# v of four pairs at once with the sequence in the partitions, twelve merge gates moved into the pairs

## The chip, the cores and the metric

The kernel runs on one core of a Trainium2 chip. The core has five engines that work side by side: TensorE (PE, matmuls into PSUM banks), VectorE (DVE), ScalarE (ACT), GpSimd (POOL) and SyncE (SP), whose queue issues nearly all DMAs of this kernel, in order. The metric is the time of one execution on the device in microseconds (us), as the median of several runs.

## The reference

One layer of a decoder with three branches; sequence 1024, width 1024, float32:

```python
h = rms_norm(x, norm_g[l])
proj = jnp.einsum('bsd,dn->bsn', h, w_in[l])
(a_val, a_glu, a_gate, b_q, b_f, b_i, b_gate,
 c_q, c_k, c_v, c_gate, c_f, merge) = jnp.split(proj, split_points, axis=-1)
ya = conformer_conv(a_val, a_glu, ...) * jax.nn.silu(a_gate)
yb = hgrn2(b_q, b_f, b_i, lower_bounds[l], hgrn_norm_g[l]) * jax.nn.silu(b_gate)
yc = forgetting_attention(c_q, c_k, c_v, c_f + fox_f_bias[l], ...) * jax.nn.silu(c_gate)
branches = jnp.stack([ya, yb, yc], axis=2)
branch_d = jnp.einsum('bskc,kcd->bskd', branches, w_branch[l])
gates = jax.nn.sigmoid(merge.reshape(B, S, N_BRANCH, D_MODEL))
x = x + jnp.einsum('bsd,de->bse', jnp.sum(gates * branch_d, axis=2), w_out[l])
```

Branch a is a causal depthwise convolution of width 31 with a LayerNorm over the channels behind it, branch b a gated linear recurrence (hgrn), branch c attention with a forget gate. c_v and b_i are the "v" of branches c and b. The merge gates are 3 x 1024 columns of the projection.

## The kernel before

**Jobs.** h is kept transposed (channels in the partitions) as a high and a low part, hT_hi and hT_lo. A projection of 128 columns is a *job*: 48 matmuls of 128x512, in two halves of 24 (high x high, high x low, low x high, for eight blocks of channels). Its weights are loaded by `fetch` (tile wraw, 512 KB) and taken apart by `split`: ScalarE copies the high part whi, VectorE subtracts to get the low part wlo; each of the three tiles has two buffers. `lin` walks through the list of 137 full jobs in order. Their results rotate over three PSUM banks, bank0 to bank2, one per half, so a half can start when the half three before it is out of its bank.

**Stages.** First eight pairs (head pair c of attention with head c of hgrn), eight jobs each: q, k, v and gate of c, then q, f, v and gate of b. Then the convolution (glu and val, eight channel blocks), mixed with the merge gates m_c and the branch matmuls br_c; then m_b and br_b; then the gates of branch a (ag0 to ag7), m_a0 to m_a7, br_a0 to br_a7; at the end the output projection.

**What runs beside the jobs.** Coroutines (attention `att`, `hgrn`, the turning of v `vprep`, `conv`, `lnstats`, `yload`) issue their steps in between. A planner (`Sched`) with costs per engine decides when each goes on, and a scheduler then sets the final order of every engine. Free tiles of 128x1056 come from a pool `F` of 18; a tile can be given out again only when its last readers, stores among them, are done.

**v.** A v job leaves v with channels in the partitions; `v_done` copies it out of the banks, `vprep` turns it by eight 128x128 transposes on TensorE into two extra banks, and ScalarE copies it out again. Then attention or hgrn of that pair starts.

**Convolution and LayerNorm.** `conv` takes 31 steps per channel block on VectorE, adds the result to a sum and stores it in zdram. `lnstats` follows the last block: GpSimd adds the sum over the partitions (`partition_all_reduce`, line 928), ScalarE makes the mean, and then each of the eight blocks is loaded, the mean is subtracted, it is stored again, squared and added up, on two tiles in turn; a second sum over the partitions (line 946) and a few steps give rs, the factor that every y of branch a is multiplied with.

**Gates of a.** `ag_done` takes each half of an ag job out of its bank by a tanh on ScalarE and an operation on VectorE; behind the second half come six more VectorE operations that need rs and end in the high and low part of that block, yhi and ylo.

**Branches.** `yload` brings yc (and later yb) from memory into ylo, ScalarE copies the high part to yhi, VectorE subtracts. A branch job br needs its gate (`merge_done`, tanh of an m job), and for b and a the sum so far from mdram; br_b stores its sum in mdram by halves.

**Opening.** x comes in eight tiles on SP's queue; per tile ScalarE squares, VectorE scales, TensorE turns. g8 (the norm's weights), gq, gk and fb are loaded on ScalarE's queue; g8 is turned, and VectorE copies it to gcol (line 1225).

## Time and profile before

| | us |
|---|---|
| median of 3 runs (1909.35 to 1914.12) | 1911.22 |
| the profiled execution | 1909.62 |
| its span | 1907.9 |
| TensorE busy | 1887.4 (99%) |
| VectorE busy | 1284.9 (67%) |
| ScalarE busy | 954.0 (50%) |
| GpSimd busy | 187.5 (10%) |

The stages by job starts: opening to 45 us, the pairs to 1017 (124 us each), convolution with branch c to 1378, branch b to 1553, the gates of a to 1640, m_a to 1727, br_a to 1814, output to 1908.

Busy time counts an instruction's whole record. Records of matmuls overlap, so the distance between starts says more than their length. The chain of waits goes back from the last instruction to what released each step; a wait named there is one that counted.

### The profile page before, as it was taken

The page shows a single profiled execution, that of the slowest core. Times are in us where ns is not written, and L with a number is a line of the kernel's source. Part 1 is how long each engine was busy: PE and PEld are TensorE (multiplying, and loading weights), DVE is VectorE, ACT ScalarE, POOL GpSimd, SP SyncE. Part 2 cuts the span into 40 slices and gives each one's busy share as a digit, 9 for nine tenths or more (in the row PEclk, how much of TensorE's full clock was granted, in tenths as well). Part 3 has the DMA queues.
Part 4 walks back from the last instruction along what each step waited for, and adds up shares of the span by engine and source line. Part 5 has one row for each costly group of instructions (what it writes and reads, how often), then busy time and mean ns, then how long its engine had stood idle before and what let it go on. Part 6 is the DMA issues. An engine that isn't in the chain of part 4 may idle for free.

```text
span 1907.9 us, 27045 instructions
## 1 busy us (share of the span) xinstructions
PE 1887.4 (99%) x11083; PEld 1551.7 (81%) x11083; DVE 1284.9 (67%) x1692; ACT 954.0 (50%) x1508; POOL 187.5 (10%) x164
## 2 busy tenths in 40 slices
PE   7999999999999999999999999999999999999999
PEld 6887878878878788787887888888888888888888
DVE  6566595775756857659577999999996467413431
ACT  5767768767687687776876411111121234322210
POOL 2021120211202111112021100000000110000000
PEclk9999999999999999999999999999999999999999
DMA  4111111111111111111111322222344553313441
GB/s 147 45 34 45 45 34 45 56 35 56 32 39 53 34 45 45 45 47 32 45 56 41 137 75 70 67 77 67 123 153 151 196 158 92 88 45 102 119 128 49
DMA packets 173012, 140.83 MB, mean 74 GB/s; under 512 B 4909, under 2 KB 155445, under 8 KB 172888
## 3 DMA queue, kind: packets, MB, share of 16 engines
q1 hardware_dynamic: 172520, 139.10, 23.5%
q8 instruction: 87, 1.43, 0.3%
q14 instruction: 37, 0.30, 0.0%
q10 hardware_dynamic: 368, 0.01, 0.0%
HBM read 109.72 MB, written 29.36 MB: 73 GB/s over the span
## 4 chain that ended last, share of the span: by engine, by line
PE 86%; ACT 8%; DVE 3%; DMA 2%; issue 1%; POOL 0%; DVEq 0%; SPq 0%; ACTq 0%; POOLq 0%
PE bank L111 84%; ACT fb L124 4%; ACT khi L124 2%; DVE fa L128 1%; PE bank L115 1%; DMA zdram<-fa 1%; ACT L124 1%; ACT fa L124 1%; DMA fa<-zdram 1%; ACT whi L354 0%; PE bank L1246 0%; PE bank L1223 0%; DVE wlo L355 0%; DVE fb L128 0%; DVE klo L132 0%
## 5 line engine op out<-in xcount | busy, mean ns | idle before, releaser
L111 PE MATMUL bank<-hT_hi,whi 128*128 128x512 f32 x1792 | 706.9, 394 | 0.0
L111 PE MATMUL bank<-hT_hi,wlo 128*128 128x512 f32 x1792 | 701.3, 391 | 0.6 <-DVE wlo L355 0.5
L111 PE MATMUL bank<-hT_lo,whi 128*128 128x512 f32 x1792 | 701.0, 391 | 0.0
L111 PEld LDWEIGHTS bank<-hT_hi,wlo 128*128 128x128 f32 x1792 | 336.5, 188 | 72.0 <-issue 2.4
L111 PEld LDWEIGHTS bank<-hT_hi,whi 128*128 128x128 f32 x1792 | 336.8, 188 | 69.3 <-issue 3.2
L111 PEld LDWEIGHTS bank<-hT_lo,whi 128*128 128x128 f32 x1792 | 336.9, 188 | 64.2 <-issue 0.2
L354 ACT ACTIVATE whi<-wraw 128x1024 fp32r<-128x1024 f32 x137 | 144.9, 1058 | 355.5 <-PE bank L111 341.0
L132 DVE SCALAR_TENSOR_TENSOR fa<-fa,taps,fa 128x1024 f32<-128x1024 f32 x240 | 299.1, 1294 | 0.4
L355 DVE TENSOR_TENSOR wlo<-wraw,whi 128x1024 fp32r<-128x1024 f32 x137 | 191.6, 1399 | 126.4 <-ACT whi L354 125.6
L128 DVE TENSOR_TENSOR fa<-fa,fa 128x512 f32<-128x512 f32 (+3 forms) x226 | 173.4, 782 | 66.5 <-ACT fa L124 49.6
L124 ACT ACTIVATE fa<-bank 128x512 f32<-128x512 f32 (+1 forms) x182 | 103.3, 576 | 141.3 <-PE bank L111 128.1
L111 PE MATMUL bank<-yhi,whi 128*128 128x512 f32 x384 | 149.4, 389 | 0.0
L111 PE MATMUL bank<-ylo,whi 128*128 128x512 f32 x384 | 149.2, 389 | 0.0
L111 PE MATMUL bank<-yhi,wlo 128*128 128x512 f32 x384 | 149.2, 389 | 0.0
L124 ACT ACTIVATE fb<-bank 128x512 f32<-128x512 f32 (+5 forms) x262 | 114.1, 450 | 41.2 <-PE bank L111 29.8
L128 DVE TENSOR_TENSOR fa<-fa,fb 128x512 f32<-128x512 f32 (+1 forms) x121 | 81.4, 672 | 58.9 <-ACT fb L124 37.8
L124 ACT ACTIVATE fb<-bank,negF,rk 128x256 f32<-128x256 f32 (+1 forms) x184 | 89.2, 549 | 49.1 <-PE bank L111 33.4
L124 ACT ACT_TABLE_LOAD x83 | 106.5, 1283 | 4.3 <-DVE fb L128 2.9
L132 DVE SCALAR_TENSOR_TENSOR fa<-fa,bank 128x512 f32<-128x512 f32 x96 | 65.4, 682 | 59.8 <-PE bank L111 59.7
L124 ACT ACTIVATE fa<-fa 128x256 f32<-128x256 f32 (+3 forms) x109 | 75.8, 720 | 53.4 <-DMA zdram<-fa 28.2
L124 ACT ACTIVATE fb<-fb 128x1024 f32<-128x1024 f32 (+2 forms) x96 | 88.1, 952 | 16.1 <-DVE fb L128 15.1
L111 PEld LDWEIGHTS bank<-yhi,wlo 128*128 128x128 f32 x384 | 72.1, 188 | 15.1
(163 smaller groups left out, 2136.1 us busy)
## 6 DMA issues: line engine op xcount, KB each, us to landing
wraw<-in_w_in_dram SPq DMA_DIRECT2D x113, 512.0 KB, 3.7
wraw<-in_w_branch_dram SPq DMA_DIRECT2D x24, 512.0 KB, 3.7
zdram<-fa SPq DMA_DIRECT2D x16, 512.0 KB, 4.0
mdram<-fa SPq DMA_DIRECT2D x32, 256.0 KB, 2.0
fa<-mdram SPq DMA_DIRECT2D x16, 512.0 KB, 3.5
fa<-zdram SPq DMA_DIRECT2D x16, 512.0 KB, 3.3
...
```

Source lines behind the costliest of these rows:

```text
L111: self.nc.tensor.matmul(out, lhsT=lhsT, rhs=rhs, start=start, stop=stop)
L115: self.nc.tensor.transpose(out, in_, ident)
L124: return self.nc.scalar.activation(out, in_, func, **kw)
L128: self.nc.vector.tensor_tensor(out=out, in0=a, in1=b, op=op)
L132: self.nc.vector.scalar_tensor_tensor(out=out, in0=a, scalar=s, in1=b, op0=op0, op1=op1)
L354: pin(nc.scalar.activation(j.hi, j.raw, AF.Copy))
L355: pin(eng.tensor_tensor(out=j.lo, in0=j.raw, in1=j.hi.bitcast(F32), op=ALU.subtract))
```

## The change

- **v.** Four jobs of a new kind, all in the first pair, replace the 16 v jobs. A `VJob` makes v of four pairs of one branch: the stationary side is a block of hT (128 positions of the sequence), the moving side 512 columns of weights. Its weights are loaded, copied and subtracted by `vfetch` in eight tiles of F; `vgroup` runs eight groups of 24 matmuls. The result has the sequence in the partitions and goes to memory (vdram). Each pair loads its v from there in `g_pre`, and attention and hgrn of a pair start there. `vprep` is gone.
- **Gates.** The twelve jobs m_b2 to m_b7 and m_a2 to m_a7 run inside pairs 1 to 7 (pairs 1 to 5 take two, 6 and 7 one) and their tanh is stored in gdram; `br_pre` loads it. So a pair has eight jobs up to pair 5, and seven in the last two (counted from 0).
- **hgrn's keys** are turned by seven transposes, not eight.
- **Opening.** g8, gq, gk and fb are loaded on SP's queue, between the tiles of x; the turn of g8 and the copy to gcol stand behind the scaling of the fourth tile.

The diff, cut:

```diff
+    def vfetch(j):
+        yield need(KT + 2)
+        j.lo = [F.get(dt=F32R, w=S) for _ in range(4)]
+        j.hi = [F.get(dt=F32R, w=S) for _ in range(4)]
+        for n, (lo, hi) in enumerate(zip(j.lo, j.hi)):
+            raw = F.get()
+            nc.sync.dma_start(out=raw[:, 0:S].rearrange("p (k c) -> p k c", k=2),
...
+                nc.scalar.activation(hi[:, 0:S], raw[:, 0:S], AF.Copy)
+                nc.vector.tensor_tensor(out=lo[:, 0:S], in0=raw[:, 0:S],
...
+    def vgroup(j):
+        w = lambda ts, k: ts[k // 2][:, k % 2 * H2:(k % 2 + 1) * H2]
+        for i in range(KT):
+            if i % 2 == 0:
+                yield need(1)
+                ot = F.get()
+            ps = ps_lin()
+            for k in range(KT):
+                hh, hl = (h[:, k, i * P:(i + 1) * P] for h in hT)
+                sc.mm(ps, hh, w(j.hi, k), k == 0, False, 228)
+                sc.mm(ps, hh, w(j.lo, k), False, False, 228)
+                sc.mm(ps, hl, w(j.hi, k), False, k == KT - 1, 228)
...
+            sc.act(ot[:, i % 2 * H2:(i % 2 + 1) * H2], ps, AF.Copy)
...
-    def vprep(st, tag, cb):
-        vT, V = st["vT"], st["V"]
-        yield
-        pss = yield from bget(2)
-        for k in range(KT):
-            sc.tr(pss[k // 4][:, k % 4 * P:(k % 4 + 1) * P], vT[:, k * P:(k + 1) * P], ident)
-        for half in range(2):
-            sc.act(V[:, half * H2:(half + 1) * H2], pss[half], AF.Copy)
...
+            nc.sync.dma_start(out=st["V"][:, 0:S], in_=vdram[tag, c // 4][c % 4])
+            st["v"] = True
             cb()
...
-        for ch in range(KT):
+        for ch in range(KT - 1):
             sc.tr(pss[ch // 4][:, ch % 4 * P:(ch % 4 + 1) * P], k_in[:, ch * P:(ch + 1) * P], ident)
...
+            if (b, j) in gdram:
+                yield need(1, True)
+                mg[b, j] = F.get(True)
+                nc.sync.dma_start(out=mg[b, j][:, 0:S], in_=gdram[b, j])
...
+        def done(half, hs, ps):
+            sc.act(st["t"][:, hs], ps, AF.Tanh, scale=0.5)
+            if half == 1:
+                nc.sync.dma_start(out=gdram[b, j], in_=st["t"][:, 0:S])
+                fput(st["t"])
...
-        if j + AHB < KT:
+        if j + AHB < KT and ("b", j + AHB) not in gdram:
             jobs.append(mjob("b", j + AHB))
...
-    jobs += [mjob("a", j) for j in range(KT)]
+    jobs += [mjob("a", j) for j in range(KT) if ("a", j) not in gdram]
...
+    K(nc.tensor.transpose(banks[7][:, 0:KT], g8, ident[0:KT, 0:KT]))
+    K(nc.vector.tensor_copy(gcol, banks[7][:, 0:KT]))
```

The order of three engines at three places. First VectorE's queue where rs becomes ready, before: the first row ends in rs (fa5_307), the last one empties the first half of ag0 from bank1 (fa7_348).

```order
L128 TENSOR_TENSOR fa5_307_9496<-fa5_307_9496,fa8_342_11921 128x1024
L355 TENSOR_TENSOR wlo_12159<-wraw_12084,whi_12158 128x1024
L128 TENSOR_TENSOR fa9_345_11951<-fa9_345_11951,fa3_347_12090 128x512
L128 TENSOR_TENSOR fa0_350_12177<-fa0_350_12177,fa5_307_9496 128x1024
L128 TENSOR_TENSOR fa2_354_12247<-fa2_354_12247,fa5_307_9496 128x1024
L136 TENSOR_SCALAR fa6_351_12178<-fa0_350_12177,vecs_110 128x1024
L132 SCALAR_TENSOR_TENSOR fa7_348_12175<-fa1_349_12176,bank1_77 128x512
```

The same place in the new order: the first row ends in rs (fa4_368), the last one empties the first half of ag2 from bank2.

```order
L129 TENSOR_TENSOR fa4_368_10234<-fa4_368_10234,fa7_405_12385 128x1024
L129 TENSOR_TENSOR fa0_410_12439<-fa0_410_12439,fa4_368_10234 128x1024
L129 TENSOR_TENSOR fa3_414_12509<-fa3_414_12509,fa4_368_10234 128x1024
L137 TENSOR_SCALAR fa6_411_12440<-fa0_410_12439,vecs_110 128x1024
L137 TENSOR_SCALAR fa9_415_12510<-fa3_414_12509,vecs_110 128x1024
L133 SCALAR_TENSOR_TENSOR fa6_411_12440<-fa8_409_12438,fa6_411_12440 128x1024
L133 SCALAR_TENSOR_TENSOR fa9_415_12510<-fa2_413_12508,fa9_415_12510 128x1024
L133 SCALAR_TENSOR_TENSOR fa6_411_12440<-fa6_411_12440,fa5_408_12437 128x1024
L133 SCALAR_TENSOR_TENSOR fa9_415_12510<-fa9_415_12510,fa1_412_12507 128x1024
L129 TENSOR_TENSOR fa8_418_12579<-fa8_418_12579,fa4_368_10234 128x1024
L129 TENSOR_TENSOR ylo0_9879<-fa6_411_12440,yhi0_9871 128x1024
L133 SCALAR_TENSOR_TENSOR fa7_416_12577<-fa5_417_12578,bank2_78 128x512
```

What moved: before, the first half of ag0 stood behind rs and three operations that need it; now ag0 and ag1 (fa5_408, fa1_412) are now out of their banks ahead of rs, and ag2's first half stands behind ten operations that need rs.

SP's queue around the loads of branch c (ylo), before: the store of hgrn's last result (yb) and the weights of br_c0 (in_w_branch) behind.

```order
L340 DMA wraw_9271<-in_w_in_dram 128x8x128
L964 DMA ylo0_9129<-yc_138 128x1024
L964 DMA ylo1_9130<-yc_138 128x1024
L964 DMA ylo2_9131<-yc_138 128x1024
L964 DMA ylo3_9132<-yc_138 128x1024
L964 DMA ylo4_9133<-yc_138 128x1024
L964 DMA ylo5_9134<-yc_138 128x1024
L964 DMA ylo6_9135<-yc_138 128x1024
L964 DMA ylo7_9136<-yc_138 128x1024
L340 DMA wraw_9330<-in_w_in_dram 128x8x128
L873 DMA yb_137<-fa1_277_8311 128x1024
L340 DMA wraw_9394<-in_w_branch_dram 128x8x128
```

And in the new order:

```order
L391 DMA wraw_9968<-in_w_branch_dram 128x8x128
L391 DMA wraw_10028<-in_w_in_dram 128x8x128
L907 DMA yb_137<-fb3_338_8982 128x1024
L391 DMA wraw_10086<-in_w_in_dram 128x8x128
L998 DMA ylo0_9879<-yc_138 128x1024
L998 DMA ylo1_9880<-yc_138 128x1024
L998 DMA ylo2_9881<-yc_138 128x1024
L998 DMA ylo3_9882<-yc_138 128x1024
L998 DMA ylo4_9883<-yc_138 128x1024
L998 DMA ylo5_9884<-yc_138 128x1024
L998 DMA ylo6_9885<-yc_138 128x1024
L998 DMA ylo7_9886<-yc_138 128x1024
```

What moved: the loads of ylo stood ahead of the yb store and of br_c0's weights, and now stand behind both and behind two more weight loads.

ScalarE's queue at the very start, before: eight entries ahead of the first square of x (L1230), six of them loads.

```order
L1210 DMA g8_121<-in_norm_g_dram 8x128
L253 ACT_TABLE_LOAD
L253 ACTIVATE warm_95<-eps_t_93 128x1
L1213 DMA gq_114<-in_fox_qn_g_dram 64x1
L1213 DMA gk_115<-in_fox_kn_g_dram 64x1
L1213 DMA gq_114<-in_fox_qn_g_dram 64x1
L1213 DMA gk_115<-in_fox_kn_g_dram 64x1
L1214 DMA fb_116<-in_fox_f_bias_dram 16x1
L1230 ACTIVATE fb1_10_154,ss_120<-fa0_1_145 128x1024
```

And in the new order:

```order
L254 ACT_TABLE_LOAD
L254 ACTIVATE warm_95<-eps_t_93 128x1
L1301 ACTIVATE fb1_10_170,ss_120<-fa0_1_161 128x1024
L1304 ACTIVATE ss_120<-ss_120 128x1
L1301 ACTIVATE fb1_10_170,ss_120<-fa1_2_162 128x1024
```

What moved: the six loads went to SP's queue, g8's behind the first tile of x, the others behind the fifth.

## Rows read from the trace of the kernel before

**Rows 1.** The page's first part: busy us, share of span, instructions of each engine.

```profile
PE 1887.4 (99%) x11083; PEld 1551.7 (81%) x11083; DVE 1284.9 (67%) x1692; ACT 954.0 (50%) x1508; POOL 187.5 (10%) x164
```

**Rows 2.** Busy time by stage: window, length, PE, PEld, DVE, ACT, POOL, clock, DMA.

```profile
150.00:273.00 123.00, 121.96 (x875) 98.96 (x874) 85.81 (x138) 91.89 (x154) 19.48 (x14) 1.00 0.15 44
1060.00:1460.00 400.00, 400.00 (x1771) 331.36 (x1770) 384.36 (x345) 80.45 (x96) 6.86 (x7) 1.00 0.32 104
1460.00:1553.00 93.00, 92.64 (x409) 76.39 (x407) 41.90 (x39) 22.72 (x26) 13.06 (x2) 1.00 0.51 171
```

**Rows 3.** Timeline of TensorE, two of 57 matmuls in a row: start, length, operation.

```profile
1439.83 0.39 PE L111 MATMUL bank<-hT_hi,whi 128*128 128x512 f32 x1
...
1452.52 0.39 PE L111 MATMUL bank<-yhi,wlo 128*128 128x512 f32 x1
```

**Rows 4.** Chain of waits, pieces of eight transposes: start, length, what.

```profile
258.44 0.87 PE bank L115 x8
...
1001.94 0.87 PE bank L115 x8
```

**Rows 5.** Groups by line and shape, TensorE: busy us, mean ns | idle before.

```profile
L115 PE MATMUL bank<-ident,fb 128*128 128x128 f32 x192 | 28.2, 274 | 2.0 <-ACT fb L124 2.0
```

**Rows 6.** Timelines of ScalarE and VectorE in the opening; in brackets idle time before.

```profile
6.68 0.34 ACTq L1214 DMA_DIRECT2D fb<-in_fox_f_bias_dram  x1
7.07 1.06 ACT L1230 ACTIVATE fb<-fa 128x1024 f32<-128x1024 f32 x1 [4.13 <-DMA gq<-in_fox_qn_g_dram]
...
11.68 0.20 ACT L1233 ACTIVATE ss<-ss 128x1 f32<-128x1 f32 x1 [3.46 <-DVE ss L1231]
...
11.41 0.17 DVE L1225 COPY gcol<-bank 128x8 f32<-128x8 f32 x1 [6.79 <-PE bank L1224]
```

**Rows 7.** Timelines of TensorE, VectorE and GpSimd from br_b3's end to rs.

```profile
1475.87 0.39 PE L111 MATMUL bank<-hT_hi,whi 128*128 128x512 f32 x1
...
1476.79 0.69 DVE L128 TENSOR_TENSOR fa<-fa,fa 128x512 f32<-128x512 f32 x1
...
1477.64 6.95 POOL L928 PARTITION_ALL_REDUCE fa<-fa  x1 [145.57 <-DVE fa L128]
...
1485.71 1.23 DVE L128 TENSOR_TENSOR fa<-fa,fa 128x1024 f32<-128x1024 f32 x1 [7.10 <-ACT fa L124]
...
1504.13 1.23 DVE L128 TENSOR_TENSOR fa<-fa,fa 128x1024 f32<-128x1024 f32 x1 [3.75 <-DMA fa<-zdram]
...
1545.55 1.23 DVE L128 TENSOR_TENSOR fa<-fa,fa 128x1024 f32<-128x1024 f32 x1 [4.62 <-ACT fa L124]
...
1546.87 6.11 POOL L946 PARTITION_ALL_REDUCE fa<-fa  x1 [62.28 <-DVE fa L128]
...
1560.13 1.22 DVE L128 TENSOR_TENSOR fa<-fa,fa 128x1024 f32<-128x1024 f32 x1
...
1565.27 0.80 DVE L136 TENSOR_SCALAR fa<-fa,vecs 128x1024 f32<-128x1024 f32 x1
```

**Rows 8.** Chain of waits in the rounds: store, square and load of one block.

```profile
1505.38 2.60 DMA zdram<-fa
1508.06 1.07 ACT fa L124
...
1510.41 3.33 DMA fa<-zdram
```

**Rows 9.** DMA issues: count, KB each, median us from issue to landing.

```profile
mdram<-fa SPq DMA_DIRECT2D x32, 256.0 KB, 2.0
```

**Rows 10.** Timelines of SP's queue, VectorE and TensorE around the loads of branch c.

```profile
1072.97 3.72 SPq L964 DMA_DIRECT2D ylo<-yc  x8
...
1081.83 0.32 SPq L873 DMA_DIRECT2D yb<-fa  x1
...
1094.51 3.49 DVE L128 TENSOR_TENSOR ylo<-ylo,yhi 128x1024 fp32r<-128x1024 f32 x3
...
1117.06 0.39 PE L111 MATMUL bank<-ylo,whi 128*128 128x512 f32 x1
```

More of the change, by code (lines that the diff above doesn't have):

```diff
@@ L40 @@
 ORD = "01ab"
+EARLY = [(b, j) for b in "ba" for j in range(2, 8)]
 AHB = 2
@@ L293, in build @@
     mdram = dram.tile([KT, P, S], F32, name="mdram")
+    vdram = {(t, h): dram.tile([4, P, S], F32, name=f"v{t}{h}") for t in "cb" for h in range(2)}
+    gdram = {(b, j): dram.tile([P, S], F32, name=f"g{b}{j}") for b, j in EARLY}
     def need(n, late=False):
@@ L336, in __init__ @@
             self.raw = self.hi = self.lo = None
+    class VJob:
+        pre, narrow = None, False
+        def __init__(self, src, tag, half):
+            self.src, self.tag, self.half = src, tag, half
+    def vfetch(j):
[5 more added lines that the diff above has]
+            nc.sync.dma_start(out=raw[:, 0:S].rearrange("p (k c) -> p k c", k=2),
+                              in_=j.src[n * 256:(n + 1) * 256].rearrange("(k p) c -> p k c", p=P))
+            with tc.high_priority(HP):
+                nc.scalar.activation(hi[:, 0:S], raw[:, 0:S], AF.Copy)
+                nc.vector.tensor_tensor(out=lo[:, 0:S], in0=raw[:, 0:S],
+                                        in1=hi[:, 0:S].bitcast(F32), op=ALU.subtract)
+            fput(raw)
+        sc.t["act"] += 4 * 950
+        sc.t["dve"] += 4 * 1240
+    def vgroup(j):
[10 more added lines that the diff above has]
+                sc.mm(ps, hl, w(j.hi, k), False, k == KT - 1, 228)
+                if k == 3:
+                    yield 0
+            sc.act(ot[:, i % 2 * H2:(i % 2 + 1) * H2], ps, AF.Copy)
+            if i % 2:
+                for n in range(2):
+                    nc.sync.dma_start(
+                        out=vdram[j.tag, j.half][:, :, (i - 1 + n) * P:(i + n) * P].rearrange("c p e -> p c e"),
+                        in_=ot[:, n * H2:(n + 1) * H2].rearrange("p (c e) -> p c e", c=4))
+                fput(ot)
+            yield 0
+        fput(*j.lo, *j.hi)
     def fetch(j):
@@ L364, in lin @@
             for i in {3: (3,), 5: (4,)}.get(m, (n + 2,) if n > 2 and not half else ()):
-                if i < len(jobs):
+                if i < len(jobs) and not isinstance(jobs[i], VJob):
                     fetch(jobs[i])
@@ L368, in lin @@
                 if i < len(jobs):
-                    split(jobs[i])
+                    if isinstance(jobs[i], VJob):
+                        yield from vfetch(jobs[i])
+                    else:
+                        split(jobs[i])
+            if isinstance(j, VJob):
+                if not half:
+                    yield from vgroup(j)
+                continue
             if not half and j.pre is not None:
@@ L1149, in build @@
         jobs.append(Job(col(8, c), hX, k_done(sa), k_pre(sa)))
[L1150 to L1151 removed]
+        if c == 0:
+            jobs.append(VJob(col(9, 0, 4 * P), "c", 0))
+        jobs.append(Job(col(10, c), hX, g_done(sa), g_pre(sa, "c", (lambda s: lambda: sc.start(att(s), f"att{s['c']}"))(sa))))
+        if c == 0:
+            jobs.append(VJob(col(5, 0, 4 * P), "b", 0))
+        else:
+            jobs += [pjob(*bj) for bj in early[:1]]
+            del early[0]
         jobs.append(Job(col(3, c), hX, bq_done(sb), bq_pre(sb)))
+        if c == 0:
+            jobs.append(VJob(col(9, 4, 4 * P), "c", 1))
         jobs.append(Job(col(4, c), hX, bf_done(sb), bf_pre(sb)))
[L1154 to L1155 removed]
+        if c == 0:
+            jobs.append(VJob(col(5, 4, 4 * P), "b", 1))
+        elif c < 6:
+            jobs += [pjob(*bj) for bj in early[:1]]
+            del early[0]
+        jobs.append(Job(col(6, c), hX, g_done(sb), g_pre(sb, "b", (lambda s: lambda: sc.start(hgrn(s), f"hg{s['c']}"))(sb))))
+    assert not early
     def swap():
@@ L1218, in build @@
             fetch(jobs[{3: 0, 4: 1, 7: 2}[i]])
+        if i == 0:
+            nc.sync.dma_start(out=g8, in_=norm_g.rearrange("a (k p) -> (a k) p", p=P))
+        if i == 4:
+            for h in range(2):
+                for dst, a in ((gq, qn_g), (gk, kn_g)):
+                    nc.sync.dma_start(out=dst[h * 64:(h + 1) * 64, :], in_=a[0].unsqueeze(1))
+            nc.sync.dma_start(out=fb, in_=f_bias[0].unsqueeze(1))
     nc.sync.dma_start(out=vst[0:31, 0:S], in_=conv_w[0])
@@ L1221, in build, with warmup @@
         nc.sync.dma_start(out=vst[r:r + 1, 0:S], in_=a)
-    for _ in range(NWARM):
-        nc.tensor.matmul(banks[7][:, 0:P], lhsT=ident, rhs=ident, start=True, stop=True)
-    nc.tensor.transpose(banks[6][:, 0:KT], g8, ident[0:KT, 0:KT])
-    nc.vector.tensor_copy(gcol, banks[6][:, 0:KT])
+    def warmup(n):
+        for _ in range(n):
+            K(nc.tensor.matmul(banks[7][:, 0:P], lhsT=ident, rhs=ident, start=True, stop=True))
+    warmup(NWARM)
     def x_sq(i):
```

51 lines of the change are left out of this document (17 added, 34 removed).

## The prediction

> **What bounds the kernel now.** I read the busy shares first, then the busy time by stage, then the chain of waits, and only then single engines. The shares say that TensorE is busy for 1887.4 of 1907.9 us, VectorE for 67% and ScalarE for half [rows 1]. The stages say the same of each stretch: 121.96 of the 123.00 us of a pair, all of 1060 to 1460, 92.64 of the last 93 us ahead of the a gates [rows 2]. So work taken from TensorE is worth its full time, and a new wait of TensorE costs its full time. One warning stands in the same rows: from 1060 to 1460 VectorE is busy for 384.36 of 400 us.
>
> The unit of TensorE is the start-to-start time, not the length of a record. 57 matmuls in a row stand from 1439.83 to 1452.52, 56 steps, hence 226.6 ns each, while each record is 0.39 us long [rows 3]. A job is 48 of them, 10.88 us, half a job 5.44.
>
> **What the change takes away.** In the kernel before every v is turned on TensorE by eight transposes, for 16 v's, and the keys of each hgrn pair by eight where seven are now enough. That is 128 + 8 = 136 transposes fewer. Eight in a row take 0.87 us in each of seven pieces of the chain, the first at 258.44 and the last at 1001.94 (the first pair's piece is of nine) [rows 4], so 109 ns each and 136 x 0.109 = **14.8 us**. The new v jobs have as many matmuls as the 16 they replace (4 x 8 x 24 = 16 x 48 = 768), of the same 128x512 shape, so they change nothing in that sum. The copies of v from the banks leave ScalarE, which is busy for 91.89 of 123 us there [rows 2]; that gains nothing, as TensorE is the bound.
>
> The group of these transposes shows 274 ns as mean of one [rows 5]. The Trainium skill, page "TensorE: Matmul & The Clock Gate", section "Part 4: PE-mode transpose", also gives about 275 ns for one in a kernel. By that price the removal would be worth 136 x 0.275 = 37.4 us, and the sum would come out 22.6 us lower. The trace disagrees for transposes in a row: the next one starts after 109 ns, and the 274 overlap.
>
> **The opening.** Before, ScalarE issues the small loads until 6.68 + 0.34 = 7.02, its first square starts at 7.07, and then it waits 3.46 us, until 11.68, since VectorE stands at the copy of gcol, for which it waited 6.79 us [rows 6]. In the new order the copy stands behind the fourth row scale, and ScalarE issues no load. The 3.46 us is what is clearly on the path, since the squares, scales, turns and splits that follow lead straight to the first matmul; the earlier first square might give another us, while the loads of x behind the small ones on SP's queue might eat it. I take **3.5 us**, bounds 0 and 4.5.
>
> **The v jobs in the first pair.** Each wants four loads, four copies on ScalarE and four subtractions on VectorE (1.22 us each, as an operation of that size in [rows 7]) before its first group. They have the job ahead, 10.88 us, as cover. With all of it hidden the cost is 0; with two of the four jobs uncovered it is 2 x 4 x 1.22 = 9.8. The order puts parts of the first one behind the split of the job ahead, which waits for a weight buffer, so a part shows; the other jobs seem covered. I take **3 us**.
>
> **The normalization of the convolution, the large term.** Before, six b gates stand between the b branch jobs. The chain that ends in rs (the factor that every y of branch a needs) starts when br_b3's result is out of the bank, at 1476.79 + 0.69 = 1477.48; the sum over the partitions starts at 1477.64, the first subtraction at 1485.71, four rounds of load, subtract, store, square and add run on one buffer from 1504.13 to 1545.55 + 1.23 = 1546.78, the second sum starts at 1546.87, and rs is there at 1560.13 + 1.22 = 1561.35 [rows 7]. From 1475.87, where TensorE turns from br_b3 to the next job, that is 85.5 us, covered by seven jobs of b (76.2 us) and the start of ag0. TensorE stands still there for less than one us [rows 2].
>
> Now the gates are gone from between. The convolution's last tap stands on VectorE just behind br_b4's evacuation, but the sum's tile is the one that br_b5 gives back, so the chain starts behind br_b5, and behind it TensorE has br_b6, br_b7, then the a gates. Call br_b5's end zero.
> - Its evacuation takes 1477.48 - 1475.87 = 1.6, its store of a half 2.0 us to landing [rows 7, 9]: the sum starts at 3.6.
> - The first subtraction comes 1485.71 - 1477.64 = 8.07 later: 11.7.
> - Four rounds, two buffers side by side, by the four rounds before (1546.78 - 1504.13 = 42.65): 54.4.
> - From the second sum's start to rs 1561.35 - 1546.87 = 14.5: 69.0.
> - In VectorE's new order ten operations stand between rs and the evacuation of ag2's first half (eight of 1.22, two of 0.80 [rows 7]: 11.4), then the evacuation itself, 0.7: bank2 is free at 81.1.
>
> TensorE runs through br_b6, br_b7, ag0, ag1, ag2 and half of ag3 and then needs bank2: 5.5 x 10.88 = 59.8. The wait is 81.1 - 59.8 = **21 us**. The evacuations of ag0 and ag1 stand inside the rounds, so their banks are no obstacle.
>
> Bounds: the shortest rows give a round of 1.24 + 2.60 + 1.07 + 3.33 plus gaps, 8.4 us [rows 7, 8], three of these and a last one without load 31.4, so a wait of 10. With the whole stretch of before, 1485.71 to 1546.78 = 61.1, it is 18.4 more, 39.7. I take 21, since the four rounds from 1504.13 are the ones that had two buffers.
>
> **The load of branch c.** Before, SP issues the loads of ylo from 1072.97, the result yb of hgrn's eighth pair is stored at 1081.83, and the last subtractions end at 1094.51 + 3.49 = 1098.0 [rows 10]. br_c0 needs the first of them at 1117.06 [rows 10] and the last 21 matmuls later, at 1121.8: 23.8 us in hand. Now the last pairs have seven jobs and not eight, and hgrn's last matmuls stand in m_c1 and not in val1, two jobs (21.8 us) nearer to br_c0. That leaves 2.0. Further, the loads now stand behind the yb store on SP's queue, and not 1081.83 - 1072.97 = 8.9 us ahead of it; behind that store also stands a weight load that waits for br_c0's split. 8.9 - 2.0 = **7 us** of wait for TensorE. Bounds: 0, if VectorE makes its eight subtractions back to back (8 x 1.22 = 9.8 and not 15.1), and 12, if that weight load costs another half job.
>
> **What else.** Pairs 6 and 7 and the convolution get denser: VectorE's 15.6 us of idle time in 400 [rows 2] must take in the steps of hgrn that now come later. Bounds 0 and 12; I take **2 us**, as any earlier wait of TensorE gives VectorE time to catch up. The stored gates cost twelve stores and twelve loads of 512 KB, issued a job or more ahead of use, and the v's sixteen loads: hidden behind the jobs, 0, and about 3.3 us [rows 8] for each that isn't.
>
> **The sum.** The profiled execution took 1909.6 us. 1909.6 - 14.8 - 3.5 + 3 + 21 + 7 + 2 = 1924.3. The median of the runs shown is 1911.2, 1.6 more, so I give **1926 us**, slower by 0.8%. A measurement of this kernel tells about 0.3% (5.7 us) from no change.
>
> **Rivals.**
> - *The waits are small.* The rounds run at their shortest rows (wait 10), the load of c and the v jobs are covered: 1909.6 - 18.3 + 10 + 1.6 = 1903 us, faster by 0.4%. For it: the store at 1505.38 took only 2.60 [rows 8]. Against: two buffers mean two stores and two loads at a time, and the four rounds that had them took 42.65 [rows 7]. It decides where the two waits together stay under 12.6 us. Chance 0.17, and 0.03 more for the transposes being worth 275 ns each, which gives 1926 - 22.6 = 1903 too.
> - *In between.* Both waits come out at about half, 14 and not 28 us: 1912, no change. Chance 0.17.
> - *The wait is as long as before's chain.* The rounds again take 61.1 us, as weight loads and gate loads share SP's queue, and the load of c takes 12: 1909.6 - 18.3 + 39.7 + 12 + 3 + 2 + 1.6 = 1950 us. Chance 0.11.
> - *The v jobs are slower than the v's were,* since hT's blocks are now the stationary side. No row shows a reason; at 240 ns and not 227 it is 768 x 0.013 = 10 us, 1936. Chance 0.04.
>
> The forecast itself has 0.48, with 1917 to 1940 as its own range. Together: faster 0.20, same 0.17, slower 0.63. The range that leaves some 2 in 10 out runs from 1899 to 1942.
>
> **What would show it.** Right: no transposes of v, and TensorE's stretch of a pair about 1.75 us shorter; one wait of TensorE in the a gates, ended by the evacuation of ag2 behind rs, 10 to 40 us long; a wait at br_c0's first ylo of up to 12. Wrong: TensorE without a gap in the a gates, the first sum starting well ahead of br_b5's end, or ylo finished before br_c0 starts. If the waits are there and the time is still shorter, the savings were more than I counted.

## The result, and the profile after

The changed kernel takes **1958.99 us** (median of 4 runs, 1957.2 to 1962.47) against 1910.28 before: 1.0251 times as long, 95% interval 1.0234 to 1.0269. The prediction had the sign, slower, but 1926 us is 33 us short of it, and its range ended at 1942.

The page's first part, after (before in [rows 1]): busy us, share, instructions.

```profile
PE 1889.6 (97%) x10947; PEld 1537.7 (79%) x10947; DVE 1273.0 (65%) x1692; ACT 939.4 (48%) x1475; POOL 183.6 (9%) x164
```

TensorE has 136 instructions fewer and nearly the same busy time, in a span of 1956.1 and not 1907.9 us. So nearly all of the 48 us is time in which it stands still: 66.5 us, and 20.5 before. Busy time by stage, after (columns as in [rows 2]): the first pair, pair 2, pair 7, glu0 to br_c0, branch b, the wait in the a gates, and the 7 us behind that wait.

```profile
20.00:323.00 303.00, 287.75 (x1434) 231.75 (x1435) 110.18 (x168) 126.30 (x194) 13.59 (x17) 0.97 0.26 78
439.00:562.00 123.00, 123.00 (x861) 99.64 (x860) 75.01 (x112) 89.73 (x151) 18.67 (x15) 1.00 0.22 65
1032.50:1152.80 120.30, 113.60 (x829) 90.05 (x827) 85.78 (x138) 93.03 (x158) 21.91 (x16) 1.00 0.16 49
1152.80:1265.40 112.60, 109.50 (x743) 85.73 (x742) 103.08 (x127) 43.23 (x72) 12.70 (x8) 1.00 0.22 71
1530.00:1638.80 108.80, 108.80 (x482) 90.09 (x481) 90.01 (x89) 23.08 (x25) 6.11 (x1) 1.00 0.68 226
...
1680.00:1703.00 23.00, 0.30 (x1) 0.30 (x2) 15.42 (x16) 10.38 (x11) 3.50 (x1) 0.50 0.17 55
1703.00:1710.00 7.00, 7.00 (x25) 5.62 (x25) 6.92 (x8) 1.25 (x2) 0.00 (x0) 0.79 0.05 14
```

Pair 2, with its two gates, and branch b are full. The third figure from the end of a row is the granted clock of TensorE, as a share of the full one; 0.79 is a mean, of 0.50 up to 1705.9 us and 1.00 from 1706 on. Time is lost at three places: the first pair, the a gates, and from pair 7 to branch c. TensorE's waits there, after (what waited, for whom: us in total, times, longest):

```profile
PE bank L116 <- DVE fb L485: 6.3, 1, 6.3
PE bank L1317 <- DVE fa L1314: 5.3, 1, 5.3
PE bank L1317 <- DVE ss L1302: 3.4, 1, 3.4
...
PE bank L112 <- DVE fb L133: 2.9, 2, 2.1
...
PE bank L112 <- DVE fa L133: 26.1, 1, 26.1
```

The first three stand in the first pair, the next in pair 7, the last in the a gates. A record's length hides shorter waits, so the balance is made of starts: from each matmul's start to the next, less its price. The price is 0.227 us for 512 columns ([rows 3]), 0.109 for a transpose ([rows 4]), and for other shapes about the usual step in these traces (0.174 for 384 columns, 0.12 for 256, 0.11 for 128). What is over, added up between job starts, in us (cq0 is the job q of c in pair 0; where one job ends and the next begins is not sharp, so a row is good to about one us):

| stretch | before | after | difference | predicted |
|---|---|---|---|---|
| up to cq0 | 13.9 | 8.4 | -5.5 | -3.5 |
| cq0 to cq1 (first pair with the v jobs) | 6.5 | 26.6 | +20.1 | +3 |
| cq1 to cq7 (pairs 1 to 6) | 14.4 | 17.0 | +2.6 | within "what else", 2 |
| cq7 to glu0 (pair 7) | 2.3 | 10.0 | +7.7 | the same |
| glu0 to br_c0 | 0.1 | 7.0 | +6.9 | load of c, 7, and the same |
| br_c0 to m_b0 | -0.4 | 3.3 | +3.7 | the same |
| branch b | 0.4 | -0.2 | -0.6 | 0 |
| a gates and m_a | -0.1 | 27.8 | +27.9 | +21 |
| matmuls and transposes by their own prices | 1863.4 | 1848.6 | -14.8 | -14.8 |

That is 48 us, the difference of the spans; br_a and the output, not listed, are over by nearly the same in both.

**The a gates.** Timelines of VectorE, GpSimd and TensorE, after, from br_b5's end to the end of the wait (before in [rows 7]; start, length, operation, idle time before and its releaser):

```profile
1616.77 0.69 DVE L133 SCALAR_TENSOR_TENSOR fa<-fa,bank 128x512 f32<-128x512 f32 x1 [4.03 <-PE bank L112]
1617.50 0.69 DVE L129 TENSOR_TENSOR fa<-fa,fa 128x512 f32<-128x512 f32 x1
...
1620.73 6.11 POOL L962 PARTITION_ALL_REDUCE fa<-fa  x1 [141.86 <-DMA mdram<-fa]
...
1630.12 2.35 DVE L129 TENSOR_TENSOR fa<-fa,fa 128x1024 f32<-128x1024 f32 x2
...
1675.16 1.23 DVE L129 TENSOR_TENSOR fa<-fa,fa 128x1024 f32<-128x1024 f32 x1 [3.19 <-ACT fa L125]
...
1676.48 7.01 POOL L980 PARTITION_ALL_REDUCE fa<-fa  x1 [49.64 <-DVE fa L129]
...
1690.16 3.62 DVE L129 TENSOR_TENSOR fa<-fa,fa 128x1024 f32<-128x1024 f32 x3
...
1701.97 0.68 DVE L133 SCALAR_TENSOR_TENSOR fa<-fa,bank 128x512 f32<-128x512 f32 x1
...
1676.19 0.39 PE L112 MATMUL bank<-hT_hi,wlo 128*128 128x512 f32 x1
1702.70 0.80 PE L112 MATMUL bank<-hT_hi,whi 128*128 128x512 f32 x1 [26.13 <-DVE fa L133]
```

The sum over the partitions waits for the store of branch b's result ("DMA mdram<-fa"), as predicted: its tile is br_b5's. TensorE works until half of ag3 is done and then stands until ag2's first half is out of its bank, at 1702.65. In the prediction's count, with br_b5's end, 1616.58, as zero (it stands 0.92 us ahead of the 0.69 us step of line 129, as in [rows 7]):

| | predicted | measured |
|---|---|---|
| first sum starts | 3.6 | 4.1 |
| first subtraction starts | 11.7 | 13.5 |
| the rounds end | 54.4 | 59.8 |
| rs is there (first of the three at 1690.16) | 69.0 | 74.8 |
| bank2 is free | 81.1 | 86.1 |
| TensorE blocked from | 59.8 | 59.8 |

So the wait is 26.3 and not 21; the rounds took 46.3 and not 42.65, the way from the sum to the first subtraction 9.4 and not 8.1. On that way ScalarE's step for the mean now stands behind a copy of weights (L405, 1.07 us from 1627.43), and VectorE's first subtraction behind that of the same weights. Why the rounds were longer stays open.

**The first pair.** Timelines of ScalarE, TensorE and VectorE, after:

```profile
28.37 1.06 ACT L358 ACTIVATE fa<-fa 128x1024 fp32r<-128x1024 f32 x1 [6.92 <-DMA fa<-in_w_in_dram]
...
29.43 1.04 ACT L1301 ACTIVATE fb<-fa 128x1024 f32<-128x1024 f32 x1
...
32.16 1.12 PE L1317 MATMUL bank<-ident,fa 128*128 128x128 f32 x4 [5.26 <-DVE fa L1314]
36.65 1.11 PE L1317 MATMUL bank<-ident,fa 128*128 128x128 f32 x4 [3.37 <-DVE ss L1302]
...
69.70 2.27 DVE L485 TENSOR_TENSOR_SCAN fb<-fb,fb 16x1024 f32<-16x1024 f32 x1
72.00 2.36 DVE L359 TENSOR_TENSOR fb<-fa,fa 128x1024 fp32r<-128x1024 f32 x2
...
72.03 1.03 PE L116 MATMUL bank<-ident,fb 16*128 16x16 f32 x8 [6.26 <-DVE fb L485]
```

ScalarE's queue is in order. Line 358 is the copy of the v job's first weights; it stands ahead of the squares of x's second half (L1301) and waits 6.92 us for its load. So x's second half is scaled and turned (L1317) late, and TensorE waits twice, 8.6 us. Then the first v job needs its low parts (L359), which stand on VectorE behind the running sum of the forget gate (L485); TensorE waits another 6.3 us at that place, as its own queue has that sum's turning (L116) ahead of most of the v job. Around these waits the granted clock is lower:

```profile
30.03:40.27 10.24, 4.61 (x17) 3.51 (x18) 8.62 (x26) 7.27 (x16) 0.00 (x0) 0.50 0.01 2
70.99:77.82 6.83, 5.57 (x19) 4.54 (x20) 4.79 (x5) 1.71 (x4) 0.00 (x0) 0.50 0.47 143
```

For 17 us, in and behind the waits, the granted clock is at 0.50, and matmuls of 512 columns start 0.43 us apart. Of the 26.6 us over, some 15 are waits and some 5 are such longer steps; before, the clock is at 1.00 in the whole first pair.

**The load of branch c.** Timelines of GpSimd, VectorE, SP's queue, ScalarE and TensorE, after (before in [rows 10]):

```profile
1240.53 6.41 POOL L903 PARTITION_ALL_REDUCE fb<-fa  x1 [59.66 <-ACT fa L125]
1241.53 4.91 DVE L406 TENSOR_TENSOR wlo<-wraw,whi 128x1024 fp32r<-128x1024 f32 x1
1246.36 7.26 DVE L133 SCALAR_TENSOR_TENSOR fa<-fa,taps,fa 128x1024 f32<-128x1024 f32 x6
...
1254.79 0.34 SPq L907 DMA_DIRECT2D yb<-fb  x1
1257.12 0.37 SPq L391 DMA_DIRECT2D wraw<-in_w_in_dram  x1
1257.59 4.25 SPq L998 DMA_DIRECT2D ylo<-yc  x8
...
1262.63 2.25 ACT L125 ACTIVATE yhi<-ylo 128x1024 fp32r<-128x1024 f32 x2 [10.10 <-DMA ylo<-yc]
...
1263.79 0.70 PE L112 MATMUL bank<-yhi,whi 128*128 128x512 f32 x2 [1.84 <-issue]
1265.06 0.50 PE L112 MATMUL bank<-ylo,whi 128*128 128x512 f32 x1 [0.57 <-DVE ylo L129]
1269.18 0.50 PE L112 MATMUL bank<-ylo,whi 128*128 128x512 f32 x1 [0.83 <-DVE ylo L129]
```

The loads stand behind the yb store, as the order said, and br_c0's matmuls find yhi and ylo a little late: 3.2 us in these three rows, where 7 were predicted. (The profile names no releaser for the 1.84; the first of the two copies to yhi ends just ahead of it, at about 1263.7.) The last steps of hgrn stand among the convolution's taps (L133, six in a row): 40 taps, 48 us of VectorE, run between the start of glu0 and the store of yb, 103 us later. Before, it was 21 taps, 28.5 us, and the store came 66 us behind glu0's start.

### The profile page after: what moved, and what is told of

Its sections match the earlier page's. It is cut to its first block, busy times and chain, and to the rows that moved or that the text cites. A ratio compares the mean times of both kernels' runs of the same rounds, so it can differ in the third digit from the quotient of the medians.

```text
span 1956.1 us, 26957 instructions
## 1 busy us (share of the span) xinstructions
PE 1889.6 (97%) x10947; PEld 1537.7 (79%) x10947; DVE 1273.0 (65%) x1692; ACT 939.4 (48%) x1475; POOL 183.6 (9%) x164
## 4 chain that ended last, share of the span: by engine, by line
PE 82%; DVE 7%; ACT 5%; issue 4%; DMA 1%; SPq 1%; POOL 0%; POOLq 0%; DVEq 0%; ACTq 0%
PE bank L112 81%; DVE fa L133 3%; ACT fb L125 1%; ACT fa L125 1%; DVE wlo L406 1%; ACT khi L125 1%; DVE fa L129 1%; ACT L125 1%; DMA fa<-in_w_in_dram 1%; PE bank L116 0%; POOLq L1409 0%; DVE fb L129 0%; POOL fa L962 0%; DVE fa L137 0%; DVE fb L133 0%
## 5 line engine op out<-in xcount | busy, mean ns | idle before, releaser
L112 PE MATMUL bank<-hT_hi,whi 128*128 128x512 f32 x1536 | 607.2, 395 | 28.7 <-DVE fa L133 26.1
L112 PE MATMUL bank<-hT_lo,whi 128*128 128x512 f32 x1536 | 602.3, 392 | 0.0
L112 PE MATMUL bank<-hT_hi,wlo 128*128 128x512 f32 x1536 | 601.7, 392 | 0.1
L112 PEld LDWEIGHTS bank<-hT_hi,wlo 128*128 128x128 f32 x1536 | 288.8, 188 | 63.6 <-issue 3.5
L133 DVE SCALAR_TENSOR_TENSOR fa<-fa,taps,fa 128x1024 f32<-128x1024 f32 x240 | 296.5, 1283 | 0.4
L405 ACT ACTIVATE whi<-wraw 128x1024 fp32r<-128x1024 f32 x121 | 128.1, 1059 | 308.4 <-PE bank L112 297.7
L125 ACT ACTIVATE fa<-bank 128x512 f32<-128x512 f32 (+6 forms) x246 | 120.9, 499 | 217.3 <-PE bank L112 205.9
L112 PE MATMUL bank<-fb,hT_hi 128*128 128x512 f32 x448 | 146.6, 396 | 0.2 <-DVE fb L359 0.2
L125 ACT ACTIVATE fa<-fa 128x256 f32<-128x256 f32 (+4 forms) x108 | 80.8, 765 | 53.2 <-DMA zdram<-fa 27.3
L125 ACT ACTIVATE fb<-bank 128x512 f32<-128x512 f32 (+6 forms) x166 | 79.0, 484 | 52.8 <-PE bank L112 41.8
L112 PEld LDWEIGHTS bank<-fb,hT_hi 128*128 128x128 f32 x448 | 84.2, 189 | 19.2 <-issue 0.4
L133 DVE SCALAR_TENSOR_TENSOR fa<-fa,bank 128x512 f32<-128x512 f32 x84 | 57.5, 685 | 59.9 <-PE bank L112 57.6
L125 ACT ACTIVATE fb<-bank,negF,rk 128x256 f32<-128x256 f32 (+1 forms) x168 | 80.8, 552 | 29.4 <-PE bank L112 19.9
L125 ACT ACTIVATE fb<-fb 128x1024 f32<-128x1024 f32 (+4 forms) x87 | 80.3, 945 | 23.4 <-DVE fb L129 22.7
```

What stands on the lines that cost most here:

```text
L112: self.nc.tensor.matmul(out, lhsT=lhsT, rhs=rhs, start=start, stop=stop)
L125: return self.nc.scalar.activation(out, in_, func, **kw)
L133: self.nc.vector.scalar_tensor_tensor(out=out, in0=a, scalar=s, in1=b, op0=op0, op1=op1)
L405: pin(nc.scalar.activation(j.hi, j.raw, AF.Copy))
```

## The experiments

The two theories after the result. **Cover:** the jobs that were taken from somewhere (six b gates from branch b, two v jobs a pair) were the work under which another chain ran, and each place pays. **Code of its own:** the v jobs' preparation is what costs. The edits are against the changed kernel unless said otherwise. "Over" is meant as in the table above; in the orders of jobs, V is a v job, cg the gate of c, and bq, bf, bg are q, f and gate of b.

**The wait in the a gates.** m_a0 and m_a1 (two jobs that don't need rs) ahead of the a gates:

```diff
+    jobs += [mjob("a", j) for j in range(KT) if ("a", j) not in gdram]
     for c in range(KT):
         jobs.append(Job(col(2, c), hX, ag_done(s), ag_pre(s)))
-    jobs += [mjob("a", j) for j in range(KT) if ("a", j) not in gdram]
```

> The changed kernel with m_a0 and m_a1 ahead of ag0 and not behind ag7, nothing else. Theory (the wait in the a gates is the normalization chain from br_b5's end to ag2's bank, 85.9 us in the changed kernel's trace against 59.8 us of jobs): TensorE has two jobs more ahead of that bank, 21.8 us, so the wait falls from 26.3 to about 4.5 us and the time from 1959 to about 1937. Rival (the wait is not this chain's, but hangs on ag3 itself, its weights or its tiles, and moves along with it): the wait stays near 26 and the time near 1959.

Measured: 1939.78 us, 1.0158 (1.0143 to 1.0173). TensorE's only listed wait from 1500 to 1800 us:

```profile
PE bank L112 <- DVE fa L133: 5.3, 1, 5.3
```

26.1 has become 5.3: two jobs are 21.8 us, and the time fell by 19.2. What is missing there is cover, and the chain of rs doesn't mind what covers it.

**The gates alone.** The kernel before, with the twelve gates moved and nothing else:

```diff
+EARLY = [(b, j) for b in "ba" for j in range(2, 8)]
...
-        if j + AHB < KT:
+        if j + AHB < KT and ("b", j + AHB) not in gdram:
```

> The kernel before with only the twelve gates moved into pairs 1 to 7 (ten jobs per pair in pairs 1 to 5, nine in 6 and 7); v's, keys and opening as before. Theory (moving the six b gates uncovers the normalization chain, whatever v does): a wait of about 26 us in the a gates, no wait at br_c0 since the pairs are not shorter than before, time about 1910 + 26 = 1936. Rival (the wait needs the v jobs too, as tiles or the planner's order are different without them): time within 5 us of 1910.

Measured: 1941.16 us, 1.0164 (1.0149 to 1.0179), all of it with the 16 v jobs and their transposes still there. TensorE's longest wait in it:

```profile
PE bank L112 <- DVE fa L133: 25.4, 1, 25.4
```

So this wait belongs to the gates and not to v. The seven pairs from pair 1 on, two of which now have nine jobs and five ten, pay 4.6 us more than before by the count of starts; glu0 to m_b0 pays nothing (-0.1 us, where the change pays 10.3).

**v alone.** The change with no gate moved, so that every pair from 1 on has six jobs:

```diff
-EARLY = [(b, j) for b in "ba" for j in range(2, 8)]
+EARLY = []
```

> The changed kernel with no gate moved (v jobs, keys and opening as in the change; pairs 1 to 7 have six jobs each). Theory (three separate costs): no wait in the a gates; the waits of the first pair stay (about 14 us over the kernel before); the pairs get denser than in the change, as attention and hgrn have six jobs of cover and not eight, so waits in the pairs and at br_c0 grow from some 20 us to 30 or 60: 1910 - 20 + 14 + 30 to 60 = 1934 to 1964. Rival (density costs next to nothing, what was seen in the last pairs is something else): 1910 - 20 + 14 = 1904 to 1910.

Measured: 1998.13 us, 1.046 (1.0441 to 1.0479), slower than the whole change. There is no wait for rs in the a gates here (one of 2.3 us for a weight split), but one of 13.5 in the convolution, at 1196 us, and the seven pairs of six jobs are together some 62 us more over than the pairs 1 to 7 before. Its busy times over one pair, then the chain of waits by line (share of the window) over the same pair, first in this kernel:

```profile
560.00:672.00 112.00, 102.15 (x771) 81.57 (x770) 81.18 (x131) 87.37 (x149) 23.93 (x16) 0.98 0.16 48
...
by line: PE bank L112 31.9%; DVE fa L129 18.1%; ACT fb L125 7.6%; issue 7.4%; ACT fa L125 7.0%; ACT L125 7.0%; DVE fb L129 3.1%; DVE wlo L406 2.8%; DVE gt L129 2.1%; DVE qst L129 2.1%; ACT whi L405 1.9%; DVE fb L133 1.7%; DVE sd L145 1.6%; 
```

and in the changed kernel, 562 to 685 us (two gates in the pair) and 1032 to 1153 (pair 7, one gate):

```profile
by line: PE bank L112 95.5%; PE bank L116 1.3%; ACT fa L125 1.1%; ACT khi L125 1.1%; DVE klo L133 0.6%; ACT fb L125 0.5%; issue 0.1%
...
by line: PE bank L112 43.8%; ACT fb L125 10.9%; ACT fa L125 5.8%; ACT L125 5.3%; DVE fa L129 4.7%; ACT khi L125 4.3%; DVE wlo L406 3.8%; issue 3.4%; DVE fb L129 2.9%; DVE qst L129 2.0%; DVE fb L133 1.9%; DVE fa L133 1.7%; DVE gt L129 1.3%; 
```

No engine is full in the pair of six jobs: VectorE 81, ScalarE 87 and TensorE 102 of 112 us (98 by the prices above). But the chain runs only 32% over TensorE, and for the rest from VectorE to ScalarE and back, with no load of v among its costly steps. The steady pairs of this kernel take 110.4 to 111.2 us by job starts: with six jobs beside them, attention and hgrn of one pair are a chain of about 111 us. With two gates in the pair the chain is TensorE's to 95%. With one it is already 44%. So with six jobs it is no longer TensorE's work that sets a pair's length. The clock has a part in it: over the seven pairs it is granted at 0.97 on the mean, and some 18 of the 62 us are steps at the lower level behind such waits.

**The opening and the keys alone.** The kernel before, with the small loads on SP's queue, g8's turn behind the fourth tile, and seven transposes for the keys:

```diff
-        for ch in range(KT):
+        for ch in range(KT - 1):
...
-    nc.scalar.dma_start(out=g8, in_=norm_g.rearrange("a (k p) -> (a k) p", p=P))
...
+        if i == 0:
+            nc.sync.dma_start(out=g8, in_=norm_g.rearrange("a (k p) -> (a k) p", p=P))
```

> The kernel before with only the new opening (small vectors on SP's queue, g8's turn and copy behind the fourth row scale) and seven key transposes per hgrn pair. Theory (the first weights job starts 5.5 us earlier in the changed kernel, and that gain is the opening's own): the time falls by 4 to 5.5 us for the opening and 0.9 us for the keys, to about 1904. Rival (the second half of x sets the pace, so an earlier first half is given back at the next turn of x): only the 0.9 us, time about 1908.

Measured: **1904.83 us** (median of 9 runs), 0.9973 (0.9964 to 0.9983): faster than both kernels. The first square on ScalarE, and the first matmul of the first job, in this kernel (before: 7.07 in [rows 6], and 23.66):

```profile
4.45 1.06 ACT L1233 ACTIVATE fb<-fa 128x1024 f32<-128x1024 f32 x1 [2.16 <-DMA fa<-in_x_dram]
...
19.45 0.50 PE L111 MATMUL bank<-hT_hi,whi 128*128 128x512 f32 x1
```

4.2 us from the opening, and the seven pairs from pair 1 on are 1.6 us shorter together, 0.22 for each removed transpose (with the smaller copy behind it). A wait for a weight split at the first a gate grew from 0.5 to 2.1 and takes 1.6 back. This part of the change is a gain by itself.

**v's weights behind x.** The first v job's copies and subtractions pinned (`K` keeps program order) behind the second half of x:

```diff
+            pin = K if (j.tag, j.half) == ("c", 0) else (lambda ins: ins)
...
-                nc.scalar.activation(hi[:, 0:S], raw[:, 0:S], AF.Copy)
+                pin(nc.scalar.activation(hi[:, 0:S], raw[:, 0:S], AF.Copy))
```

> The changed kernel with the first v job's four copies and subtractions pinned behind the second half of x on ScalarE and VectorE. Theory (in the opening ScalarE stood 6.92 us at a copy of v's weights that had not landed, with the squares of x behind it, and TensorE's two waits of 5.26 and 3.37 us come from that): both waits shrink to before's 1.4 to 1.7, and the time falls by 6 to 8 us to about 1952. Rival (v's weights land so late that the first v job then waits for them instead): the waits move behind the k job and the time stays within 2 us of 1959.

Measured: 1957.95 us, 1.0252 (1.0237 to 1.0267): no gain. TensorE's waits in its first pair:

```profile
PE bank L112 <- ACT fb L125: 11.5, 2, 10.7
PE bank L1318 <- DVE fa L1315: 1.6, 2, 1.4
```

The two waits for x are gone to 1.6 us, and one of 10.7 has grown at the v job, as the rival had it. It ends with the emptying of a bank on ScalarE (L125), and the v job goes on only at 71.44: its low parts now all stand behind the running sum (four L360 from 70.20 to 75.9 us on VectorE). So this other order of the two queues gains nothing. That there is too little in front of the first v job is put to the test next.

**A job in front of it.** Pair 0 in the order q, k, bq, V, cg, V, bf, V, one gate, V, bg, pinned as above; pair 1 keeps one gate only:

```diff
+            jobs.append(Job(col(3, c), hX, bq_done(sb), bq_pre(sb)))
             jobs.append(VJob(col(9, 0, 4 * P), "c", 0))
...
             jobs.append(VJob(col(9, 4, 4 * P), "c", 1))
+            jobs.append(pjob(*early.pop(0)))
...
-        else:
+        elif c > 1:
```

> The changed kernel with pair 0 in another order: q, k, bq, first v job, gate of c, second v job, bf, third v job, one gate (b2), fourth v job, gate of b, the first v job's copies and subtractions pinned as in e5c; pair 1 has one gate fewer. Theory (the first v job waits for its low parts, which stand on VectorE behind the running sum of the forget gate, so one more job ahead of it covers 10.9 us): the waits of pair 0 fall from 17 to about 6 and the time from 1959 to about 1948. Rival (the v jobs lack tiles or weights, whatever stands ahead of them): the waits only move to later v jobs, and the time stays within 3 us of 1958.

Measured: 1960.87 us, 1.0264 (1.025 to 1.0278): again no gain. The waits over 0.35 us between cq0 and cq1 fell from 17.2 to 7.1 us, as meant, but the gate had come out of pair 1, and one pair further on, where there had been none, they are 11.4. TensorE's waits from 400 to 570 us, the longest group:

```profile
PE bank L112 <- DVE fb L133: 4.9, 2, 2.8
```

**The gates in pairs 2 to 7.** Two gates each in pairs 2 to 7 and none in pair 1, so that the last pairs are full:

```diff
-        else:
+        elif c > 1:
...
-        elif c < 6:
+        elif c > 1:
```

> The changed kernel with two gates in each of the pairs 2 to 7 and none in pair 1 (in the change two in pairs 1 to 5, one in 6 and 7). Theory (the last pairs are too dense: attention and hgrn fall behind and end two jobs late, which gives the waits of pair 7, of glu0 to br_c0 and at the first ylo, some 8 + 9 + 4 us): these go, pair 1 has room as in the run with v alone, and the time falls from 1959 to about 1941. Rival (hgrn is late because it starts later behind the v jobs, not because of density): the same waits stay, time near 1959.

Measured: 1971.78 us, 1.0325 (1.031 to 1.0341). The theory fell as to the sum. Pair 7's waits went from 7.9 to 1.2 us, but behind pair 1 there are 12.2 now, and glu0 to br_c0 got worse, 12.1 for 3.6. TensorE's waits there:

```profile
PE bank L112 <- issue: 6.2, 1, 6.2
PE bank L112 <- DVE ylo L129: 5.4, 2, 4.8
```

Full last pairs don't bring hgrn's last result earlier: its store comes 116.5 us behind glu0's start, 103 in the change. 50 taps, 64 us of VectorE, run in that time, 40 in the change. So its steps stand among the taps; why the order puts more of them ahead here is not shown.

**All three together.** Edits of e1, e8 and e9:

> The changed kernel with all three repairs together: m_a0 and m_a1 ahead of ag0 (e1), pair 0 in the order of e8, and the eleven other gates two by two in pairs 2 to 7 (one in the last). If the three costs are separate they add: 1959 - 19 - 15 - 11 = 1914, within 0.3% of the kernel before. If they share a cause, less: about 1930. If the transposes saved are worth their full 14.8 us and nothing else is lost, down to 1895.

Measured: 1934.32 us, 1.0125 (1.0111 to 1.0139). The a gates wait 5.2 us and pair 0 7.4, but behind pair 1 it is 11.9 and from glu0 to br_c0 10.8.

**Pair 0 and m_a.** The edits of e1, and pair 0 in the order q, k, bq, V, cg, V, bf, V, bg, V, with the gates where the change has them:

```diff
+            vj = [VJob(col(o, 4 * h, 4 * P), t, h) for h in range(2) for o, t in ((9, "c"), (5, "b"))]
+            jobs += [q, k, bq, vj[0], cg, vj[1], bf, vj[2], bg, vj[3]]
```

> The changed kernel with two repairs and all twelve gates left in their pairs: m_a0 and m_a1 ahead of ag0 (e1), and pair 0 in the order q, k, bq, v job, gate of c, v job, bf, v job, gate of b, v job (first v job pinned as in e5c). In e8 the waits of pair 0 fell from 17 to 7 us and new ones of 11 us came in pair 2, where a gate was missing in pair 1. Theory (these new waits were the missing gate's): with both gates in pair 1 they don't come, and the time is 1959 - 19 - 10 = 1930. Rival (a pair 0 that ends sooner only hands its wait on to the next pairs): about 1940.

Measured: 1932.44 us, 1.0115 (1.01 to 1.013), 7.3 less than e1. TensorE's waits in its first pair:

```profile
PE bank L113 <- ACT fa L126: 3.1, 1, 3.1
...
PE bank L113 <- DVE fb L361: 0.6, 1, 0.6
```

With a job more ahead, the first v job is ready but for 0.6 us (L361 makes its low parts); the wait of 3.1 comes at 204 us, in the steps beside the jobs. The granted clock is 1.00 in the whole of the first pair. By the count of starts cq0 to cq1 is 13.3 over and not 26.6; pair 2 gives 7.9 of it back. So the time is near the theory's, but the rival had a large part of it: the new waits over 0.35 us of pair 2 were 11.4 with a gate missing in pair 1, and are still 7.2 with both gates there.

**Two gates behind pair 7.** e11 with one gate less in pairs 3 and 4:

```diff
-NGATES = [0, 2, 2, 2, 2, 2, 1, 1, 0]
+NGATES = [0, 2, 2, 1, 1, 2, 1, 1, 2]
```

> e11 with two gates (the last two) run behind pair 7, ahead of glu0, and pairs 3 and 4 with one gate each and not two. Theory (hgrn's last pair runs late into the convolution, so the first ylo waits): two more jobs of cover take away the waits from glu0 to br_c0 and at ylo, some 8 us, while the two pairs with seven jobs cost 0 to 20 us of new waits (e3's pairs with six jobs took 111 us each, about what seven jobs take): 1922 to 1942, and in the trace no wait at the first ylo. Rival (hgrn's last pair is held up by the convolution's steps on VectorE wherever the jobs stand): the wait at ylo stays.

Measured: 1950.21 us, 1.0213 (1.0194 to 1.0232), 17.8 more than e11. From glu0 to br_c0 it is 0.4 over and not 7.3: two jobs there do cover hgrn's end. But the stretches from pair 3 to pair 7 and the two gates behind it are 46.8 over and not 21.2: the pairs that the two jobs came from lost more.

**Only a's gates.** e11 with the b gates back between the b branches, and eight a gates moved, one in each of pairs 1 to 7 and one behind:

```diff
-EARLY = [(b, j) for b in "ba" for j in range(2, 8)]
+EARLY = [("a", j) for j in range(8)]
+NGATES = [0, 1, 1, 1, 1, 1, 1, 1, 1]
```

> The changed kernel with pair 0 as in e11, the six b gates back between the b branch jobs, and the eight a gates early, one in each pair 1 to 7 and one behind pair 7. Theory (the normalization chain is covered by the b gates alone; pairs need about 110 us for attention and hgrn, seven jobs give about as much): no wait in the a gates, waits of 1 to 2 us per pair more, time 1959 - 26 - 10 + 10 = 1933, and 1908 if seven jobs cost nothing. Rival (every job taken out of a pair comes back as a wait, as in e3): 1950 or more.

Measured: 1956.98 us, 1.0246 (1.023 to 1.0261). The a gates wait for nothing (0.1 us over), but pairs 1 to 7 are 75.1 over and not 33.0 as in e11: five jobs fewer in them, 42 us more. The pairs and the gate behind them in e13, then the pairs in e11 (columns as in [rows 2]):

```profile
314.11:1152.80 838.69, 803.35 (x5580) 635.77 (x5579) 560.53 (x892) 611.36 (x1006) 144.52 (x102) 0.98 0.17 53
...
313.48:1144.19 830.71, 816.39 (x5587) 655.79 (x5586) 546.79 (x854) 602.61 (x996) 133.52 (x98) 1.00 0.19 58
```

Some 21 of the 42 us are longer waits, and some 14 are steps at the lower clock, which is granted for about 37 us in these pairs and for 3 in e11. The later pairs of seven jobs take about 120 us here, more than the chain's 111 of e3 and than TensorE's own 109. So the chain's length is a floor and not the price; what makes the rest of the waits stays open.

## Why the prediction was wrong

- **The bound** was read rightly: TensorE was full, and every wait cost its full time. But that reading has a second half that I didn't take: [rows 2] gives 121.96 of 123 us of a pair to TensorE, and from that nothing follows on how long the pair would be with less of TensorE's work. The chain beside it, 111 us long where e3 lays it open, was out of sight.
- **The transposes** (-14.8): the 136 are gone. But a pair of eight jobs got only 0.8 us shorter (123.1 by job starts, 123.9 before) and not about 1.75. Whether each was worth 0.109 us stays open. The one run in which a pair lost just a transpose, e4b, gained 0.22 us for each, together with a shorter copy. The Trainium skill, page "TensorE: Matmul & The Clock Gate", section "Part 4: PE-mode transpose", gives about 275 ns for one in a kernel, more than either. If one were worth more than 0.109, the waits in the balance would be larger by as much, so this can't be the cause of a time above the forecast.
- **The opening** (-3.5, bounds 0 and 4.5): -5.5 in the change, -4.2 alone. Right in place; the first square at 4.49 and not 7.07 gave the rest.
- **The v jobs in the first pair** (+3, measured +20.1): the step that failed is "They have the job ahead, 10.88 us, as cover ... the other jobs seem covered". It set eight operations against one job as if ScalarE and VectorE were free for them. At that point both have x's second half and the forget gate's running sum in order ahead or behind. The one other order of these queues that was tried, e5c, doesn't help; e11 shows that one job more in front takes 13 us away. Of the 20.1, some 12.5 are waits, 5 the lower clock that comes with them, and 2.6 a slightly longer step of the v jobs. The term had no place for the clock.
- **The normalization** (+21, measured 27.9): the mechanism was right in each step (the tile of br_b5, the ten operations behind rs, bank2, half of ag3). Mis-sized were the rounds, 46.3 for 42.65, and the way from the sum to the first subtraction, 9.4 for 8.1; and the first eight steps behind the wait ran at the lower clock, 1.6 us.
- **The load of branch c** (+7): some 3.2 us at br_c0's first matmuls, within the bounds, smaller than I took.
- **What else** (+2, bounds 0 and 12): this is the other failed step. The table's rows from cq1 to m_b0 hold 20.9 us, of which the load of c is 3.2. I looked for the price in VectorE's idle time, as if an engine had to be full for the pairs to wait. e3 shows the waits with VectorE at 81 and ScalarE at 87 of 112 us: it is the chain between them, and pair 7 with its one gate (10.0 over) and the stage behind it (7.0) are too short for it. e8, e9, e12 and e13 took jobs out of one place for another, and each time the place that gave them, or the pair behind it, paid in waits: 11.4, 12.2, 25.6 and 42 us.
- **The rivals.** "The wait is as long as before's chain" (1950) was nearest to the time by luck: its wait came out at 26 and not 40, its load of c at 3 and not 12. "The v jobs are slower" fell as to the size: steps shorter than 0.1 us over the price add up to 2.6 us more than before in that stretch, 3.4 ns for each of 768 matmuls and not 13. The rival that was missing is that TensorE's removed work was cover in the pairs as well as in branch b.

What stays open: why the order puts so many taps ahead of hgrn's last result, even when pair 7 is full (e9), and why pairs of seven jobs take 120 us (e13). And no run has all places covered at once; there are not enough jobs that can move freely for it among those tried.
